# Layer 1's context values and keys, moved from the experts' stage to the first rows of block 2

## The chip, the cores and the metric

One core of one Trainium2 chip runs the whole program in one launch. The time is the device time in microseconds; a lower one is better. The engines are PE (TensorE, matmuls and transposes), ScalarE (ACT), VectorE (DVE), GpSimd (POOL), and SyncE (SP), which issues nearly all DMAs. Each engine works through its own instructions in a fixed order and waits on semaphores of the others.

## The reference

Two blocks of a network, one after the other, on 1024 latent rows and 256 context rows of width 1024, all in float32.

Block 1 mixes the latent rows (a Hyena filter and a gated linear recurrence, started from a context's states), adds the result, and then runs a mixture of experts over the latent rows:

```
aff = softmax(h @ router_w);  gates, idx = top_k(aff.T, 128)     # 16 experts, 128 rows each
y = (silu(xg @ w1) * (xg @ w3)) @ w2                             # w1, w3: 1024 x 2048, w2: 2048 x 1024
x = x + g2 * scatter_add(y * gates);  x = rmsnorm(x, final_g)
```

Block 2 has two layers. Each layer normalises the latent rows and a second context's 256 rows, projects them with `w_in` (1024 x 3072: Fourier and pool inputs, queries, keys, values, gate), lets the latent rows attend to the context's and the latent's keys and values, and adds the gated, projected result to the rows:

```
if update_ctx:  pc = hc @ w_in                        # layer 0
else:           pkv = hc @ w_in[:, K_OFF:G_OFF]       # layer 1: the context's keys and values alone
k_ctx = rms_norm(split_heads_qk(kc), qk_norm_g[1]);  v_ctx = split_heads_v(vc)
k_all = concat([k_ctx, k_lat]);  v_all = concat([v_ctx, v_lat])
```

Layer 1's context keys and values need the context rows after layer 0 and nothing of the latent rows. They are 256 x 512 each, in four heads of 128.

## The kernel before, in words

Matmuls of float32 precision are made of three: a matrix is split into a high half (`cp`, ScalarE) and a low half, the difference (`tt`, VectorE, or GpSimd where `eng` says so); `mm3` (lines 188 to 190) adds high x high, high x low and low x high in PSUM. A weight tile of 128 x 1024 is therefore loaded by SP (`wr`, `er`), copied by ScalarE (`wh`, `eh`) and subtracted by VectorE or GpSimd (`wl`, `el`) before PE can use it.

**The experts** (`moe`). For each of 16 experts `prep` gathers 128 rows by an indirect DMA of GpSimd, `up` makes a 128 x 512 block of both products from eight weight tiles each of `w1` and `w3` in four steps, `down` multiplies it by `w2`. Four such units an expert, 64 in all, read 768 weight tiles through `er` (10 buffers), `eh` and `el` (4 each). At an expert's end the two halves of `yo` are scaled on VectorE and added to `acc` in HBM by an indirect DMA of GpSimd (line 1265).

**The context beside them** (`ctx_rest`). `side_by_side` lays a second stream into the text of the experts: `ctx_rest` with a weight of 1/50 a step against 1/64 a step of the experts, so that its last step stands at some two fifths of them. It does layer 0's attention of the context, its output projection, which writes the new context rows to `xc` in HBM, and then the part that this document calls the tail: `ctx_hT(1)` loads `xc` (tile `cx`), normalises, transposes and scales it into `Tc`, high and low halves; `v_rows` makes the values of all heads from four weight tiles; `ctx_qk` makes the keys of a head from one weight tile each, normalises them and stores them. Its PSUM tiles are `cp` and `cm`, one bank each, its temporaries `cv` and `cu`, and its low halves are subtracted on GpSimd.

**Block 2's head.** `lat_pools` opens the weight and temporary tiles of the latent path (`wr` 2, `wh` 4, `wl` 4, `u2` 9) and PSUM (`pp` 3 banks, `pm` 1). `first_rows` then takes 256 rows at a time from `acc`: loads two tiles `r4`, squares them (ScalarE, into PSUM `fp`), scales them by `final_g` and stores them, normalises them again into `xn`, transposes them, and writes the halves to `T0`. `lat_path` follows: for layer 0 the values of the latent rows (`v_rows` with `rows_first`, four weight tiles held at once, two row tiles after two), then the queries and keys of each head, with the Fourier and pool work (`side_ct`) beside heads 1 and 2. Its `side_ct` tiles lie where those of `first_rows` were.

**Order.** The order of instructions on an engine isn't the program's. A scheduler goes through the program with a model of durations and puts on each engine's list the instruction that is ready first in the model, and among ready ones that which stands first in the program. Tiles of a pool that lies over a closed one's memory wait for the tiles that were there. The lists are fixed then; on the chip each engine keeps to its list.

Of the kernel before, what the change touches and what calls it, by code (L numbers as in the profile page):

```python
# [114 lines left out]
class Work:  # L115
# [1312 lines left out]
        self.dma(V, self.dvc[0, h])  # L1428
        return KA, lambda qb: (QA, QB), V, self.rqc[h]

    def ctx_qk(self, l, q, h, hT, w="w"):

        dst = self.dqc[h] if q == 0 else self.dkc[l, h]
        if q == 0:
            self.rqc.append(self.cst([128, 2, 2], name="rqc"))
        self.qk_rows(l, q, h, hT, 256, lambda t0, x: self.dma(dst, x), "cp", "cu", None, None if q else self.rqc[h],
                     w=w, eng=self.nc.gpsimd, pq="cm")

    def lat_operands(self, l, h):
        KA = [self.t("KA", [128, 1280], F32R) for _ in range(2)]  # L1440
# [362 lines left out]
    def ctx_rest(self):  # L1803

        dyc, dgc = self.dyc, self.dgc
        P_ = self.nc.gpsimd
        with ExitStack() as e:
            self.open(e, "right", cKA=4, cQA=6, cV=2, cE0=2, cE1=2, cth=2, cot=1)
            s0 = self.cst([128, 4, 2], name="s0")
            for h in range(4):  # L1810
                yield from self.attention(0, 256, 256, self.ctx_operands(h), dyc[4 + h], s0[:, h], "c")
        with ExitStack() as e:
            self.open(e, "right", cy=4)
            y = self.gated_y(0, 0, dyc, dgc, s0, "cp", "cy", "Tc", "cv")
            gb = self.t("cy")
            self.dma(gb, self.m2[0, 1, 2 * D:].partition_broadcast(128))
            xs = []
            for i in range(2):
                x = self.t("cy")
                self.dma(x, self.I["ctx_2"][0, i * 128:i * 128 + 128, :])  # L1820
                xs.append(x)
            yield
            for u in range(4):
                us = slice(u * 256, u * 256 + 256)
                wp = [self.wsplit(self.I["w_out_2"][0][q * 512:q * 512 + 512, us].rearrange("(k p) n -> p k n", p=128), (4, 256), "w", P_) for q in range(2)]
                for i in range(2):
                    is_ = slice(i * 128, i * 128 + 128)
                    ps = self.ps("cp", [128, 256])
                    for k in range(8):
                        wh, wl = wp[k // 4]  # L1830
                        self.mm3(ps, y[0][k // 4][:, k % 4, is_], y[1][k // 4][:, k % 4, is_], wh[:, k % 4], wl[:, k % 4], k == 0, k == 7)
                    t = self.t("cu", [128, 256])
                    self.tt(t, ps, gb[:, us], MUL)
                    self.tt(xs[i][:, us], xs[i][:, us], t, ADD, P_)
                    if u == 3:
                        self.dma(self.xc[i * 128:i * 128 + 128, :], xs[i])
                    yield
        with ExitStack() as e:
            self.open(e, "right", cx=2)
            hT = self.ctx_hT(1)  # L1840
            yield
        self.v_rows(1, 256, hT, self.dvc[1], "cp", "cv", "w", P_)
        yield
        for h in range(4):
            self.ctx_qk(1, 1, h, hT)
            yield

    def new_hT(self, tag):
        return [[self.t(tag, dt=F32R) for _ in range(8)] for _ in range(2)]
# [98 lines left out]
def side_by_side(*streams):  # L1948

    todo = [[-lead / total, total, list(gens)] for lead, total, gens in streams]  # L1950
    while todo:
        s = min(todo, key=lambda t: t[0])
        g, w = s[2][0]
        if next(g, todo) is todo:
            s[2].pop(0)
            if not s[2]:
                todo.remove(s)
        else:
            s[0] += w / s[1]


def run(K):
    fst = ExitStack()
    with ExitStack() as e1:
        K.open(e1, "left", ar=3, ah=4, al=4)
        K.open_ps(e1, "left", pp=3, mp=1)
        K.open(e1, "left", u2=4, T=16)
        K.open_ps(fst, "right", pf=4)
        K.open(fst, "right", f4=7, fb=5)
        with ExitStack() as e2:  # L1970
            K.open(e2, "right", cr=6, x=4, c=2, mr=4)
            K.start()
        K.open(fst, "right", y=3, t=4, H=2, hs=3, dc=2, ri=7, ra=2, mr=1)
        K.load_dft()
        K.mods_first()
        side_by_side((30, 450, [(K.filter_time(), 2.4), (K.filter_spectra(), 2.1), (K.hyena(), 5)]),
                   (0, 64, [(K.hy_proj(), 1), (K.hg_proj(), 1)]),
                   (0, 4, [(K.mods_layer(0, "mp", "u2", ("mr",), False), 1)]))
    fst.close()
    with ExitStack() as cx:  # L1980
        with ExitStack() as e1:
            K.open_ps(e1, "left", ph0=3, ph1=3)
            K.open(e1, "left", hmk=1, hS=2)
            for p in "01":
                K.open(e1, "left", **{"hi" + p: 6, "hw" + p: 5, "h2" + p: 3, "hm" + p: 4, "hT1" + p: 2, "hT2" + p: 4})
            K.ctx_state()
            for h in range(4):
                K.hgrn_head(h)
            K.open(cx, "right", wr=2, wh=2, wl=2, cu=6, cv=2, Tc=4, lg=2)
            K.pfx = "c"  # L1990
            with ExitStack() as e2:
                K.open_ps(e2, "right", cp=1, cm=1)
                K.open(e2, "right", mr=1)
                for _ in K.mods_tail("cm", "cv", ("wr", "wr", "mr"), False):
                    pass
                K.ctx_first()
                K.ctx_side()
                for _ in K.mods_layer(1, "cm", "cv", ("wr", "wr", "mr"), False):
                    pass
        K.open_ps(cx, "right", cp=1, cm=1)  # L2000
        K.pfx = "o"
        em = cx.enter_context(ExitStack())
        with ExitStack() as e0:
            K.open_ps(e0, "left", pp=3, pq=2, pi=1)
            with ExitStack() as e1:
                K.open(e1, "left", xm=3, rw=1, wo=16, m4=3, yt=6, u2=3)
                K.out_proj()
            K.open(em, "left", el=4, eh=4, er=10)
            with ExitStack() as e1:
                K.open(e1, "left", twr=2, twh=2, twl=2)  # L2010
                K.open(e1, "left", aff=1, tk=12, tp=2, af=4)
                K.topk()
                K.pfx = "c"
                K.ctx_heads("tw")
        with ExitStack() as e1:
            K.open_ps(e1, "left", et=1, ea=3, ey=2)
            K.open(e1, "right", g2b=1, xg=1, xf=1, xh=4, sa=4, hh=4, yo=2)
            side_by_side((0, 64, [(K.moe(), 1)]), (CL, CT, [(K.ctx_rest(), 1)]))
    K.pfx = ""
    with ExitStack() as e1, ExitStack() as e0, ExitStack() as ec:  # L2020
        K.open(e0, "right", T0=16)
        rope = K.lat_pools(ec)
        hT = K.first_rows()
        K.lat_path(hT, rope, ec, e0, e1)


class Kern:
# [9 lines left out]
    def start(self):  # L2037
        W = self.work
        W.pc, W.psm, W.pd, W.one = self.pc, self.psm, self.pd, self.one
        run(W)  # L2040
# [119 lines left out]
```

## Time and profile before

| | |
|---|---|
| time, median of 3 runs | 3869.8 us (3867.06 to 3873.09) |
| the profiled execution | 3865.27 us, span 3863.5 us |
| PE busy in the span | 3548.4 us (92%) |
| VectorE, ScalarE, GpSimd busy | 2722.9, 2224.8, 1125.8 us |
| HBM | 669.00 MB read, 107.05 MB written, 201 GB/s over the span |
| experts' weights asked for by SP | from 1183.7 to 2508.2 us |
| the tail's work on the rows `cx` and `Tc`, and its last store of keys | 1581.3 us to 1747.2 us |
| first and last matmul of layer 0's latent values | 2552.6 to 2613.7 us |

Times in rows are microseconds from the start of the span. `x` before a number counts instructions, unless it is the column of a matmul's shape. A matmul's duration in a row overlaps with the next one's; what a matmul costs PE is the distance from one start to the next. `<-` in brackets names what an engine waited for before an instruction, with the time it waited. PEld is PE's loading of weights, which overlaps with matmuls.

### The profile page before, as it was taken

The numbers are of one execution on the slowest core, as the hardware profiler recorded it, in microseconds if no ns is written. First come the engines' busy times: TensorE is split into PE (matmuls) and PEld (weight loads), VectorE is DVE, ScalarE is ACT, GpSimd is POOL, SyncE is SP. The second block draws the span as 40 slices with busy tenths as digits, with TensorE's granted clock in tenths as the row PEclk, the third lists the DMA queues.
The fourth block names the chain that finished last, engine by engine and source line by source line (L and its number), as shares of the span: only waits on it lengthen the run. The fifth ranks groups of instructions, "written<-read, shape, count | busy, mean of one in ns | idle before, by whom it ended". The sixth has DMA issues, their size and how long they took to land. (4 is left out here: it accounts for less than half of the span.)

```text
span 3863.5 us, 50949 instructions
## 1 busy us (share of the span) xinstructions
PE 3548.4 (92%) x17554; PEld 2851.0 (74%) x17554; DVE 2722.9 (70%) x4119; ACT 2224.8 (58%) x3595; POOL 1125.8 (29%) x702
## 2 busy tenths in 40 slices
PE   5998999968997899999999999979999899999989
PEld 2666878747866678787777777768778688877767
DVE  3588677787635888799888888856576744476762
ACT  4432322354434886777777777755576754456772
POOL 3355324364323213121112111001333610133361
PEclk8999999988997999999999999989999999999999
DMA  6765444363475799999999999952321143231133
GB/s 213 220 224 176 133 139 139 127 232 124 164 229 192 233 335 336 323 327 346 369 363 355 368 364 353 364 194 80 114 64 52 51 150 120 69 122 57 42 104 115
DMA packets 503020, 780.49 MB, mean 202 GB/s; under 512 B 35026, under 2 KB 238824, under 8 KB 502505
## 3 DMA queue, kind: packets, MB, share of 16 engines
q1 hardware_dynamic: 496136, 755.74, 57.3%
q0 software_dynamic: 5600, 20.43, 2.0%
q8 instruction: 138, 2.26, 0.2%
q10 hardware_dynamic: 1024, 1.06, 0.1%
q14 instruction: 122, 0.99, 0.1%
HBM read 669.00 MB, written 107.05 MB: 201 GB/s over the span
## 5 line engine op out<-in xcount | busy, mean ns | idle before, releaser
L171 DVE TENSOR_TENSOR el<-er,eh 128x1024 fp32r<-128x1024 f32 x763 | 950.6, 1294 | 112.5 <-ACT eh L168 109.4
L168 ACT ACTIVATE eh<-er 128x1024 fp32r<-128x1024 f32 x768 | 783.2, 1057 | 126.4 <-PE ea L190 92.7
L189 PE MATMUL ea<-el,xh 128*128 128x512 f32 x1024 | 415.8, 406 | 22.7 <-DVE el L171 20.2
L188 PE MATMUL ea<-eh,xh 128*128 128x512 f32 x1024 | 403.7, 397 | 1.9 <-ACT eh L168 1.9
L190 PE MATMUL ea<-eh,xh 128*128 128x512 f32 x1024 | 404.7, 395 | 0.0
L1488 DVE TENSOR_SCALAR_CACHE_REDUCE E<-s,rq 128x512 f32<-128x512 f32 (+1 forms) x384 | 237.3, 657 | 80.1 <-PE s L193 74.4
L1265 POOL DMA_INDIRECT acc<-yo,idx x16 | 71.1, 4444 | 733.8 <-DVE yo L180 726.7
L189 PEld LDWEIGHTS ea<-el,xh 128*128 128x128 f32 x1024 | 192.8, 188 | 91.3 <-DVE el L171 51.0
L165 ACT ACTIVATE E<-E,a 128x1280 f32<-128x1280 f32 x160 | 216.7, 1359 | 61.5 <-DVE a L1492 56.0
L193 PE MATMUL s<-KA,QA 128*128 128x512 f32 (+1 forms) x768 | 207.7, 394 | 32.2 <-DVE E L1488 31.1
L188 PEld LDWEIGHTS ea<-eh,xh 128*128 128x128 f32 x1024 | 192.9, 188 | 47.1 <-ACT eh L168 2.9
L190 PEld LDWEIGHTS ea<-eh,xh 128*128 128x128 f32 x1024 | 193.2, 189 | 37.6
L189 PE MATMUL ey<-el,hh 128*128 128x512 f32 x512 | 206.8, 404 | 6.4 <-DVE el L171 6.3
L188 PE MATMUL ey<-eh,hh 128*128 128x512 f32 x512 | 204.4, 405 | 7.4 <-ACT eh L168 7.3
L190 PE MATMUL ey<-eh,hh 128*128 128x512 f32 x512 | 203.6, 398 | 0.0
L171 POOL TENSOR_TENSOR wl<-wr,wh 128x1024 fp32r<-128x1024 f32 (+1 forms) x48 | 116.6, 2436 | 293.6 <-ACT wh L168 258.0
L168 ACT ACTIVATE u<-pp 32x512 f32<-32x512 f32 (+2 forms) x212 | 124.2, 586 | 112.1 <-PE pp L190 94.8
L193 PEld LDWEIGHTS s<-KA,QA 128*128 128x128 f32 x768 | 132.1, 199 | 74.6 <-DVE E L1488 55.0
L188 PE MATMUL pp<-T,ah 128*128 128x512 f32 x448 | 182.5, 407 | 2.0 <-ACT ah L168 2.0
L193 PE MATMUL po<-th,V 128*128 128x256 f32 x640 | 170.1, 391 | 13.7 <-ACT th L168 13.6
L190 PE MATMUL pp<-T,al 128*128 128x512 f32 x448 | 178.7, 399 | 0.0
L189 PE MATMUL pp<-T,ah 128*128 128x512 f32 x448 | 178.4, 398 | 0.0
(507 smaller groups left out, 8960.2 us busy)
## 6 DMA issues: line engine op xcount, KB each, us to landing
er<-in_exp_w_dram SPq DMA_DIRECT2D x768, 512.0 KB
wr<-in_w_in_dram SPq DMA_DIRECT2D x60, 512.0 KB
ar<-in_w_in_dram SPq DMA_DIRECT2D x64, 256.0 KB
mr<-in_w_mod_dram SPq DMA_DIRECT2D x30, 512.0 KB
wr<-in_ada_w_dram SPq DMA_DIRECT2D x24, 512.0 KB
wr<-in_w_out_dram SPq DMA_DIRECT2D x24, 512.0 KB
Hd<-hs SPq DMA_DIRECT2D x72, 128.0 KB
H<-Hd SPq DMA_DIRECT2D x36, 256.0 KB
```

The costliest lines, as they stand in the source:

```text
L165: return self.nc.scalar.activation(out, in_, func, **kw)
L168: return self.nc.scalar.activation(out, in_, AF.Copy)
L171: return (eng or self.nc.vector).tensor_tensor(out, a, b, op=op)
L188: mm(out, lh, rh, start=first, stop=False)
L189: mm(out, lh, rl, start=False, stop=False)
L190: mm(out, ll, rh, start=False, stop=last)
L193: self.nc.tensor.matmul(out, l, r, start=first, stop=last)
L1265: nc.gpsimd.indirect_dma_start(out=self.acc, out_offset=x[0], in_=yo, in_offset=None, compute_op=ADD)
L1488: nc.vector.tensor_scalar(E[:, k0:k1], o, r, None, op0=MUL, op1=ALU.min, accum_out=mx[:, m, j:j + 1] if nc_ > 1 else mc)
```

## The change

The tail leaves `ctx_rest`, which ends with the store of `xc`. It becomes a function of its own, `ctx_tail`, called behind `first_rows` and ahead of `lat_path` in the program. It uses the latent path's tiles (`pp`, `pm`, `u2`, `wr`, `wh`, `wl`) in place of the context's, with its low halves still on GpSimd. Two pools, `Tc` (4) and `cx` (2), 24 KB a partition, are opened below those of `first_rows` and closed behind the tail.

```diff
-    def ctx_qk(self, l, q, h, hT, w="w"):
+    def ctx_qk(self, l, q, h, hT, w="w", pt="cp", tmp="cu", pq="cm"):
...
-        self.qk_rows(l, q, h, hT, 256, lambda t0, x: self.dma(dst, x), "cp", "cu", None, None if q else self.rqc[h],
-                     w=w, eng=self.nc.gpsimd, pq="cm")
+        self.qk_rows(l, q, h, hT, 256, lambda t0, x: self.dma(dst, x), pt, tmp, None, None if q else self.rqc[h],
+                     w=w, eng=self.nc.gpsimd, pq=pq)
...
-        with ExitStack() as e:
-            self.open(e, "right", cx=2)
-            hT = self.ctx_hT(1)
-            yield
-        self.v_rows(1, 256, hT, self.dvc[1], "cp", "cv", "w", P_)
-        yield
+
+    def ctx_tail(self):
+
+        hT = self.load_h(self.xc, 256, self.A_2[1][:, 1], self.sh_2[1][:, 1], "Tc", "pp", "u2", "cx")
+        self.v_rows(1, 256, hT, self.dvc[1], "pp", "u2", "w", self.nc.gpsimd)
         for h in range(4):
-            self.ctx_qk(1, 1, h, hT)
-            yield
+            self.ctx_qk(1, 1, h, hT, "w", "pp", "u2", "pm")
...
         rope = K.lat_pools(ec)
-        hT = K.first_rows()
+        with ExitStack() as e2:
+            K.open(e2, "left", Tc=4, cx=2)
+            hT = K.first_rows()
+            K.ctx_tail()
         K.lat_path(hT, rope, ec, e0, e1)
```

## Rows read from the trace of the kernel before

**Rows 1.** Stretches: PE, PEld, DVE, ACT, POOL busy; clock, DMA share, GB/s.

```profile
1562.00:1750.00 188.00, 180.20 (x879) 147.87 (x878) 161.47 (x151) 144.32 (x190) 36.02 (x18) 0.97 0.94 320
1800.00:2500.00 700.00, 685.51 (x3010) 540.53 (x3009) 618.16 (x570) 530.24 (x614) 97.62 (x27) 1.00 1.02 361
```

**Rows 2.** The same stretches, PE's instructions on `ea` alone: busy, clock, DMA.

```profile
1562.00:1750.00 188.00, 107.68 (x415) 0.97 0.94 320
1800.00:2500.00 700.00, 454.82 (x1856) 1.00 1.02 361
```

**Rows 3.** The same for `ey`.

```profile
1562.00:1750.00 188.00, 53.92 (x192) 0.97 0.94 320
1800.00:2500.00 700.00, 232.47 (x926) 1.00 1.02 361
```

**Rows 4.** Waits, 1800 to 2500: who waited for whom, us, times, longest.

```profile
ACT eh L168 <- PE ea L190: 47.1, 89, 2.2
PEld ea L189 <- DVE el L171: 36.3, 59, 1.8
```

**Rows 5.** Groups by line and form, 1562 to 1750: count, busy us, mean ns.

```profile
L171 POOL TENSOR_TENSOR wl<-wr,wh 128x512 fp32r<-128x512 f32 x8 | 15.3, 1930 | 19.3 <-ACT wh L168 11.5 <-PE ey L190 7.7
L165 ACT ACT_TABLE_LOAD x8 | 10.3, 1283 | 0.1
...
L190 PE MATMUL cp<-Tc,wl 128*128 128x256 f32 x32 | 9.0, 281 | 0.0
...
L171 POOL TENSOR_TENSOR wl<-wr,wh 128x1024 fp32r<-128x1024 f32 x2 | 4.9, 2469 | 72.6 <-ACT wh L168 72.6
...
L196 PE MATMUL cp<-ident,cx 128*128 128x128 f32 x16 | 3.4, 294 | 0.2 <-ACT cu L165 0.2
...
L193 PE MATMUL cm<-cu,bd 128*128 128x256 f32 x8 | 2.4, 378 | 0.0
```

**Rows 6.** Timeline of PE: start, duration, what, idle time before it.

```profile
2549.04 3.92 PE L196 MATMUL fp<-ident,xn 128*128 128x128 f32 x16 [22.92 <-DVE xn L176]
...
2552.98 0.41 PE L189 MATMUL pp<-wl,T 128*128 128x256 f32 x1
2553.19 0.41 PE L188 MATMUL pp<-wh,T 128*128 128x256 f32 x1
...
2555.09 0.28 PE L189 MATMUL pp<-wl,T 128*128 128x256 f32 x1
2555.21 0.28 PE L190 MATMUL pp<-wh,T 128*128 128x256 f32 x1
...
2613.61 0.28 PE L189 MATMUL pp<-wl,T 128*128 128x256 f32 x1
```

**Rows 7.** Stretches at block 2's head, columns as in rows 1.

```profile
2526.00:2549.00 23.00, 0.12 (x1) 0.00 (x0) 9.55 (x13) 11.08 (x23) 1.55 (x1) 0.53 0.86 274
...
2550.00:2600.00 50.00, 45.47 (x349) 42.74 (x347) 31.27 (x65) 35.74 (x103) 0.35 (x2) 0.95 0.45 148
```

**Rows 8.** Timeline of ScalarE behind the last expert.

```profile
2526.33 1.06 ACT L168 ACTIVATE wh<-wr 128x1024 fp32r<-128x1024 f32 x1 [5.29 <-DMA wr<-in_w_in_dram]
...
2535.08 1.06 ACT L168 ACTIVATE wh<-wr 128x1024 fp32r<-128x1024 f32 x1 [4.56 <-DMA wr<-in_w_in_dram]
2537.41 0.60 ACT L165 ACTIVATE fp<-r 128x512 f32<-128x512 f32 x1 [1.28 <-DMA r<-acc]
```

**Rows 9.** Timeline of SP's DMA queue there.

```profile
2533.76 2.39 SPq L161 DMA_DIRECT2D r<-acc  x5
```

**Rows 10.** Timeline of GpSimd: two subtractions of the tail; the last scatter-add.

```profile
1673.43 4.50 POOL L171 TENSOR_TENSOR wl<-wr,wh 128x512 fp32r<-128x512 f32 x2
...
2527.19 1.55 POOL L1265 DMA_INDIRECT acc<-yo,idx  x1 [51.04 <-DVE yo L180]
```

**Rows 11.** Timeline of VectorE: three subtractions, beside the tail and alone.

```profile
1671.36 7.65 DVE L171 TENSOR_TENSOR el<-er,eh 128x1024 fp32r<-128x1024 f32 x3 [0.18 <-ACT eh L168]
...
2514.56 3.49 DVE L171 TENSOR_TENSOR el<-er,eh 128x1024 fp32r<-128x1024 f32 x3
```

## The prediction

> **What bounds the kernel now.** I read the busy time by stretches first, because the change takes work out of one stage and puts it into another, and the shares of the whole span say nothing about either. Two stretches of the experts' stage stand side by side [rows 1]: 1562 to 1750 us, in which the context tail (layer 1's context rows, values and keys) runs beside the experts, and 1800 to 2500 us, in which the experts run alone. In both PE is busy for about 96 to 98% and the DMA engines for 94 to 102%, so the reader cannot tell from busy shares what the tail costs. What tells it is progress: how many of the experts' matmuls PE got through. Alone the stage does 1856 up and 926 down matmuls in 700 us, 3.974 a us; with the tail beside it 415 and 192, 607 in 188 us, 3.229 a us [rows 2, 3]. At the rate of the stage alone 607 matmuls take 152.7 us. The tail therefore cost the experts 188 - 152.7 = 35.3 us.
>
> The waits of the stretch without the tail say which resource holds that rate [rows 4]. ScalarE waits for PE to give back a high half (47.1 us), PE's weight loads wait for VectorE's low half (36.3 us), and no engine is shown waiting for an expert weight to land. It is the hand-over round PE, at PE's pace, and not the DMA queue, although the queue looks full.
>
> The second stage is the beginning of block 2. The timeline of PE [rows 6] shows it standing still for 22.92 us between the last expert's matmul and the first transpose of block 2: last result, scatter-add [rows 10], reload of the rows [rows 9], two normalisations [rows 8]. After that PE is busy for 45.47 of 50 us [rows 7]: the matmuls of layer 0's latent values, which follow the rows as they come, fill it until 2613.5. So there are about 22.9 + 4.5 = 27.4 us of PE idle here, most of it in one piece.
>
> **The change, part by part.** *Out of the experts' stage.* Six groups of 32 matmuls with 256 columns, 0.118 us from start to start at the full clock (2555.09 to 2555.21) [rows 5, 6], are 192 x 0.118 = 22.7 us; 16 transposes 1.9 (an estimate: half of the 0.245 us each that 16 take at the half clock [rows 6]), the key norms' eight records 2.4: 27.0 us of PE. The rest of the 35.3 us is what it does to the hand-over: eight table loads of ScalarE, 10.3 us, because the tail's square roots alternate with the experts' Silu [rows 5], and a VectorE held up by GpSimd (below). Lower bound 27 us (PE time alone), upper 36 (the whole lost progress, plus two weight splits that lay ahead of 1562). I take **34 us**: the experts' own rate behind 1750 is seen in this trace and nothing else runs there, so I am near the measured loss.
>
> *Into the head of block 2.* Where can it start? Its PSUM tiles (`pp`, `pm`) and weight tiles come from the pools of the latent path, which lie over the experts' own, so it can't start before the experts give those back; its two row tiles lie beside them and can be loaded earlier. ScalarE does its last expert copy at about 2521 and is idle for 5.29 us [rows 8]. The granted clock in the idle stretch is 0.53 [rows 7], so PE starts there at the lower of its two levels, 1.2 of 2.4 GHz. From there: one normalisation, half of the 11.6 us that two took from 2537.41 [rows 8] to 2549.04 [rows 6], 5.8 us; then transposes at the slow clock, 16 in 3.92 us [rows 6]. PE starts the tail near 2528 and has all its rows near 2537.
>
> The weights are slower than the rows. All go through the two `wr` tiles: four tiles of values, four of keys, and only then the four for layer 0's latent values, which had the ring to themselves before. In the trace a wr tile's copy on ScalarE starts at 2526.33 and the third, which needs the first one's buffer back, at 2535.08, 8.75 us later [rows 8]: load, copy 1.06, subtraction 1.22 on VectorE. With the tail's subtraction on GpSimd (2.47 us for a value tile, 2 x 1.93 for a key tile [rows 5]) a buffer's round is about 10 to 11 us, and two buffers give a tile every 5.2 us. The first is usable at 2530 (2526.33 + 1.06 + 2.47), the second 3 us later, the third about 2538.5, the fourth waits on SP behind the five row loads of 2533.76 [rows 9] and comes near 2545. The 96 value matmuls then end near 2550: half of them at full clock 5.7 us, the others partly at the half clock, where the step is 0.21 us (2552.98 to 2553.19) [rows 6]. So the transposes and values lie inside the old 22.92 us of idle. The keys come at 2548, 2553, 2558 and 2564, and their 11.4 + 2.4 us of PE lie behind it. The latent values' weights follow; I put the first pair at 2571. In that time PE also does the first rows' transposes, as before.
>
> From there 384 latent value matmuls x 0.118 = 45.3 us, and about 4 us of transposes and gaps: they end near 2621, where they ended at 2613.6 before [rows 6]: 7 us. The path over the first rows gives a second end: their last part was ready near 2602 (2613.6 less 96 x 0.118), and may become up to 7 us later without being felt. I take **8 us**, one for small things. Bounds: 0 if all of the tail fits into the 27.4 us of idle, 27 if nothing of its PE time does.
>
> *GpSimd against VectorE.* In the tail of before, VectorE's three subtractions at 1671.36 took 7.65 us, while GpSimd ran its two at 1673.43; three alone took 3.49 [rows 10, 11]. So the tail's eight splits, 4 x 2.47 + 4 x 3.86 = 25 us of GpSimd, now meet the first rows' VectorE work. If each costs the first rows its whole length, they are 25 us late, 2613.6 + 25 is the end, and the cost is 25 in place of 8: that is a rival, below. But VectorE was busy for only 9.55 + 31.27 us of the 73 us in the two stretches of [rows 7]; it has the room, and 7 us of delay are free, so I add nothing. The Trainium skill (SBUF — State Buffer, "SBUF: two separate sides") has this as an exclusive lock on a port pair that VectorE and GpSimd share: whichever starts first holds it for its whole instruction. This trace agrees, with 7.65 against 3.49 us; by that rule in full the cost would be the 25 us of the rival.
>
> *Other moves.* The two row loads, the eight weight loads and eight stores stand in SP's queue among the latent path's; the five row loads of the first rows wait for the scatter-add, so what stands behind them there waits with them, and I have counted it for the fourth tile. The square roots now stand among other square roots: the table loads go. The side work's weight tiles, which lie over the tail's `Tc` tiles, are first loaded behind 2590, after the tail. Pushing the first rows' tiles up by 24 KB puts them over experts' tiles that end with the scatter-add for which they wait anyway. All that costs nothing; without this cover each would be one load's wait, 5 us.
>
> **The sum.** The profiled execution took 3865.3 us, span 3863.5. 3865.3 - 34 + 8 = 3839.3. The median of the runs is 3869.8, 4.5 us above that execution, so the median should come to **3844 us**.
>
> **Rivals.** *The DMA queue holds the experts' stage* (10%). For it: the DMA share of 1.02 [rows 1]. Against it: no wait on a landing [rows 4]. Then only bytes count: eight tiles of 128 x 1024 f32 (0.52 MB), two row tiles and eight small stores, 6.3 MB, at 361 GB/s 17 us. 3865.3 - 17 + 8 + 4.5 = 3861.
>
> *The weight ring* (14%): the two wr buffers turn more slowly than I have it, so that twelve tiles before the latent values make PE wait and nothing of the tail is hidden. For it: two buffers, and a round of 8.75 us that was already longer than its parts. Against it: two loads are always on the way. 34 gained, 27 lost: 3863.
>
> *Slower* (8%): in the queues' fixed order the tail stands ahead of the first rows' transposes, and the ring serves one tile at a time. One mechanism: PE can't pass a key matmul that waits for its weights, so block 2 begins when the twelfth tile has come. At 8.75 us a tile that is 12 x 8.75 = 105 us behind 2521, 2626, where the latent values began at 2553 before: 73 us late, of which 16 are won back, since from 2553 to 2613.6 they had 61 us for 45.3 us of matmuls. 3869.8 - 34 + 57 = 3893. It decides from a loss of 34 + 8 us, a tile every 7.5 us. Against it: PE ran transposes and value matmuls by turns as each got ready, so the order isn't the program's [rows 6, 7].
>
> *VectorE behind GpSimd* (6%): the first rows give up all 25 us of the tail's splits, worked out above: 3869.8 - 34 + 25 = 3861. That the change does nothing, the tail running beside the experts as before, is excluded: its PSUM isn't free until they end.
>
> **How the numbers follow.** The forecast has 62%; its own range is 3834 (36 gained, 0 lost) to 3855. A difference of 0.2%, 7.7 us, is about what a measurement of this kernel can tell from none. Faster by more than that is below 3862: all of the forecast, and some two thirds of the DMA, ring and GpSimd cases (30% together), rounded down: 0.8. Same: the other third of them, 0.12. Slower: the slow case, 0.08. The range is 3832 to 3864: it takes in the three nearer rivals and leaves out the slow one.
>
> **What would show it.** In the changed profile: no `Tc` work between 1562 and 1750, and the experts at about 3.97 matmuls a us there; the last expert matmul near 2492 instead of 2526; the eight table loads gone; the old 22.92 us of idle broken up by `pp` matmuls on `Tc`; the latent values ending some 94 us behind the start of the last scatter-add, where it was 86.4 (2527.19 to 2613.6). The prediction is wrong if the experts' last matmul moves by less than 25 us (step one), or if the latent values end more than 105 us behind the scatter-add (step two).

## The result, and the profile after

The changed kernel takes 3893.07 us (median of 4 runs, 3889.14 to 3899.96); the kernel before, run beside it, 3868.43. The ratio is 1.0073, 95% interval 1.0059 to 1.0087: 25 us slower by the medians, where 26 us faster were forecast. The profiled execution has a span of 3887.4 us, 23.9 more than before.

Two differences make these 23.9 us. The last scatter-add of the experts starts at 2485.53 us, where it was 2527.19 [rows 10]: 41.7 us earlier. The latent values of layer 0 end at 2636.3, where it was 2613.6 [rows 6]; that is 150.8 us behind the scatter-add instead of 86.4: 64.4 lost. What follows the latent values takes 1251.1 us instead of 1249.9. -41.7 + 64.4 + 1.2 = 23.9.

**The experts are free of the tail.** The stretches, columns as in [rows 1] (busy us with counts of PE, PEld, DVE, ACT, POOL; clock, DMA share, GB/s):

```profile
1562.00:1750.00 188.00, 184.63 (x813) 146.01 (x812) 166.04 (x152) 144.82 (x169) 24.03 (x8) 1.00 1.03 371
1800.00:2450.00 650.00, 636.90 (x2797) 502.63 (x2796) 575.07 (x530) 492.62 (x568) 87.53 (x24) 1.00 1.02 361
2484.00:2507.00 23.00, 0.46 (x2) 0.03 (x1) 5.46 (x8) 10.10 (x23) 8.13 (x4) 0.54 0.79 251
2507.00:2560.00 53.00, 16.76 (x71) 13.96 (x72) 36.54 (x74) 36.01 (x108) 3.52 (x4) 0.50 0.32 111
2560.00:2590.00 30.00, 29.11 (x226) 27.61 (x224) 11.54 (x22) 15.78 (x37) 10.31 (x9) 0.98 0.48 139
2590.00:2640.00 50.00, 48.70 (x390) 47.58 (x391) 13.70 (x17) 13.35 (x23) 0.00 (x0) 1.00 0.44 129
```

The first of these stretches again, with the instructions on `ea` and then on `ey` alone (PE first, then PEld, DVE, ACT), as [rows 2, 3]:

```profile
1562.00:1750.00 188.00, 123.40 (x505) 93.07 (x503) 7.53 (x11) 6.61 (x11) 1.00 1.03 371
```

```profile
1562.00:1750.00 188.00, 62.05 (x247) 45.72 (x247) 2.98 (x4) 1.00 1.03 371
```

505 + 247 = 752 matmuls in 188 us are 4.00 a us, the 3.97 of the stage alone and not the 3.23 of before. The DMA share is 1.03 at that rate, so that the queue doesn't hold the experts to the rate of before.

**Block 2's head is not.** PE's timeline answers to [rows 6]: start, duration, what, idle time before it.

```profile
2484.06 0.40 PE L190 MATMUL ey<-eh,hh 128*128 128x512 f32 x1
2508.12 1.09 PE L196 MATMUL fp<-ident,xn 128*128 128x128 f32 x4 [23.66 <-DVE xn L176]
2510.78 3.10 PE L196 MATMUL fp<-ident,xn 128*128 128x128 f32 x12 [1.57 <-DVE xn L176]
2524.07 3.93 PE L196 MATMUL fp<-ident,xn 128*128 128x128 f32 x16 [10.19 <-DVE xn L176]
2538.62 3.92 PE L196 MATMUL fp<-ident,xn 128*128 128x128 f32 x16 [10.62 <-DVE xn L176]
2555.24 1.94 PE L196 MATMUL fp<-ident,xn 128*128 128x128 f32 x8 [12.69 <-DVE xn L176]
2556.97 0.85 PE L196 MATMUL pp<-ident,cx 128*128 128x128 f32 x3
...
2562.98 0.39 PE L188 MATMUL pp<-wh,Tc 128*128 128x256 f32 x1
...
2587.47 0.28 PE L190 MATMUL pp<-Tc,wl 128*128 128x256 f32 x1
2587.59 0.28 PE L188 MATMUL pp<-wh,T 128*128 128x256 f32 x1
...
2636.26 0.28 PE L190 MATMUL pp<-wh,T 128*128 128x256 f32 x1
```

The reader is to see three things. The 22.92 us of idle ahead of the first transposes are still there, whole (23.66). Behind them the first rows come 14.5 to 16.6 us apart, about as before, but between their transposes PE now stands still for 10 to 13 us each time, where the latent values ran before: 16.76 us of work in 53, at a granted clock of 0.50, the lower level, where [rows 7] had 45.47 of 50 at 0.95. And the tail begins only with the last of the first rows, so that three pieces of work stand one behind the other: the first rows to 2560, the tail to 2587.5, the latent values to 2636.3.

ScalarE's timeline, as [rows 8], shows how the tail came there:

```profile
2495.66 0.60 ACT L165 ACTIVATE fp<-r 128x512 f32<-128x512 f32 x1 [6.71 <-DMA r<-acc]
...
2548.91 0.60 ACT L165 ACTIVATE fp<-r 128x512 f32<-128x512 f32 x1 [1.61 <-DVE r L180]
...
2549.54 0.58 ACT L165 ACTIVATE fp<-r 128x512 f32<-128x512 f32 x1
2550.06 0.19 ACT L165 ACTIVATION_READ_ACCUMULATOR fp<-r 128x1 f32 x1
2550.15 0.58 ACT L165 ACTIVATE pp<-cx 128x512 f32<-128x512 f32 x1
...
2551.99 0.58 ACT L165 ACTIVATE fp<-r 128x512 f32<-128x512 f32 x1
```

The first square of the tail's rows stands on ScalarE's list inside the eighth and last normalisation of the first rows, behind two of its four squares (2548.91 and 2549.54; the third comes at 2551.99), and waits there for nothing: `cx` had been loaded at 1566. Ahead of the first rows ScalarE was idle for 6.71 us; a tail's square didn't stand there.

SP's queue shows what the latent values waited for. These are its loads of `wr` tiles behind the scatter-add:

```profile
2494.33 0.98 SPq L161 DMA_DIRECT2D wr<-in_w_in_dram  x2
...
2508.47 0.38 SPq L161 DMA_DIRECT2D wr<-in_w_in_dram  x1
...
2511.18 0.38 SPq L161 DMA_DIRECT2D wr<-in_w_in_dram  x1
...
2574.07 0.55 SPq L161 DMA_DIRECT2D wr<-in_w_in_dram  x1
```

From 2511.18 to 2574.07 no `wr` tile was loaded. ScalarE's next copy of a weight tells why:

```profile
2570.73 1.15 ACT L168 ACTIVATE wh<-wr 128x512 fp32r<-128x512 f32 x2 [3.98 <-PE pp L190]
```

The tail's four value tiles were split by 2511 and held all four `wh` and `wl` until PE had used them; two key tiles filled both `wr`; the latent values' tiles stood behind those.

### The profile page after: what moved, and what is told of

Read it like the earlier page. It is cut to its first block, busy times and chain, and to the rows that moved or that the text cites. A ratio compares the mean times of both kernels' runs of the same rounds, so it can differ in the third digit from the quotient of the medians.

```text
span 3887.4 us, 50959 instructions
## 1 busy us (share of the span) xinstructions
PE 3544.4 (91%) x17554; PEld 2844.1 (73%) x17554; DVE 2715.0 (70%) x4119; ACT 2216.8 (57%) x3587; POOL 1128.1 (29%) x702
## 5 line engine op out<-in xcount | busy, mean ns | idle before, releaser
L171 DVE TENSOR_TENSOR el<-er,eh 128x1024 fp32r<-128x1024 f32 x763 | 936.8, 1280 | 108.2 <-ACT eh L168 104.5
```

Of the source, the lines that this page charges most:

```text
L171: return (eng or self.nc.vector).tensor_tensor(out, a, b, op=op)
```

## The experiments

My theory had two parts. **S:** a tail called behind the first rows is late because of small tiles. `row_rstd` takes `s2` and `ss`, four buffers each, and the first rows, ahead in the program, take eight `s2` before the tail takes one. **H:** once the tail is late, its value tiles hold the weight ring, and the latent values can't run beside the first rows. The rival **T:** the tail is late merely because it stands behind in the program.

What the traces showed, in us behind the start of the last scatter-add (which is at 2527.2, 2485.5, 2485.8, 2487.0, 2490.5, 2483.9, 2482.7 and 2491.5 in this order), with the medians and the ratio to the kernel before, run beside each (3868.43 us for the changed kernel, 3867.3 for e1 to e4, 3866.1 for e5 and e6):

| kernel | tail's first square | tail's last key matmul | last transpose of first rows | latent values end | median, us | ratio, 95% |
|---|---|---|---|---|---|---|
| before | in the experts | in the experts | 72 | 86 | see above | |
| after | +65 | 102 | 74 | 151 | 3893.07 | 1.0073 (1.0059 to 1.0087) |
| e1 own small tiles | -10 | 48 | 95 | 110 | 3850.92 | 0.9958 (0.9945 to 0.9972) |
| e2 no tail | | | 76 | 90 | 3832.28 | 0.9912 (0.9897 to 0.9927) |
| e3 tail first | -10 | 47 | 89 | 104 | 3842.94 | 0.9930 (0.9916 to 0.9943) |
| e4 latent values first | +74 | 117 | 73 | 86 | 3867.09 | 0.9994 (0.9984 to 1.0003) |
| e5 e3, VectorE splits | -10 | 40 | 91 | 106 | 3854.97 | 0.9972 (0.9960 to 0.9984) |
| e6 e4 with own small tiles | +74 | 117 | 74 | 86 | 3859.79 | 0.9983 (0.9974 to 0.9992) |

**e1, small tiles of the tail's own.** The tail stays where it is in the program; its small tiles get a name of their own, and so buffers of their own.

```diff
             hT = K.first_rows()
+            K.pfx = "c"
             K.ctx_tail()
+            K.pfx = ""
```

> The changed kernel, with other names for the tail's small tiles alone (sums of squares and roots: cs2 and css in place of s2 and ss, which the first rows use). Theory S: the four buffers of s2 and ss are given out in the program's order, and the tail's come behind the eight of the first rows, so its first square had to wait for their last one (2550 us). Then with own names the first square on cx runs within 10 us of the experts' last copy, at 2475 to 2490, the values' matmuls stand inside the idle time ahead of block 2's first transpose, and the time is 3868 - 42 + 8 to 20 = 3834 to 3846. Rival T: the tail is late because it stands behind the first rows in the program. Then nothing changes: first square near 2550, 3893 us.

Measured: 3850.92 us, 42 less than the changed kernel, by two lines that change no arithmetic and no order in the program. The tail's rows are squared 74 us sooner, ahead of the last scatter-add:

```profile
L165 ACT ACTIVATE pp<-cx x4: 577/582/603, 2475.8 to 2478.6; 128x512 f32<-128x512 f32 x4
```

```profile
L188 PE MATMUL pp<-wh,Tc x32: 278/283/583, 2490.2 to 2518.9; 128*128 128x256 f32 x32
```

The second row is the tail's values. They begin 4 us behind the scatter-add, in the idle time that the forecast gave them, but end 33 us behind it, where the forecast had 23 (2550). S holds and T falls: the place in the program is the same. The time is somewhat above the range expected.

The names themselves came with the change. Among the experts the tail's small tiles carried the prefix `c` too; the call behind `first_rows` stands where the prefix is empty, so that the tail took the first rows' `s2` and `ss` without a line that says so. The first of these rows is from the kernel before, the second from the changed one, where one of the nine is the tail's (the kernel before has eight):

```profile
1601.81 0.29 ACT L165 ACTIVATE css<-css,eps 128x2 f32<-128x2 f32 x1
```

```profile
L165 ACT ACTIVATE ss<-ss,eps x9: 278/295/296, 2499.6 to 2554.5; 128x2 f32<-128x2 f32 x9
```

What e1 doesn't tell is whether the number of buffers or the order in which one name is given out held the tail. By the number, four, the tail's `s2` needs only the fifth normalisation's to come back, and in the changed kernel VectorE read that one at 2532.30:

```profile
2532.30 0.16 DVE L171 TENSOR_TENSOR ss<-s 128x2 f32<-128x2 f32 x1 [0.18 <-ACT fp L165]
```

The tail's first square came 18 us later, right behind the eighth normalisation's first two. That fits the order better than the number; more buffers under one name weren't tried.

**e2, no tail at all.** Layer 1 reads the context's values and keys of layer 0; its own are not made.

```diff
-        self.dma(V[:, 0:2], self.dvc[l, h])
+        self.dma(V[:, 0:2], self.dvc[0, h])
...
-        self.dma(kc, self.dkc[l, h])
+        self.dma(kc, self.dkc[0, h])
...
-            K.open(e2, "left", Tc=4, cx=2)
+            pass
             hT = K.first_rows()
-            K.ctx_tail()
```

> The changed kernel without the tail: layer 1 reads layer 0's context values and keys in its place, and its two pools are not opened. What the experts' stage gives and what the rest of block 2's head takes without it. If all of the loss is the tail's and what it holds up: the experts end as in the changed kernel, the latent values end 86 us behind the last scatter-add as in the kernel before, and the time is 3868 - 42 = 3826 (3822 to 3831). If the head of block 2 became longer for another reason, it stays above 3840.

Measured: 3832.28 us. This is the floor, and it gives the tail's price in each place as a distance from it: 35 us among the experts (interval of the ratio, times 3867: 28 to 40), 61 in the changed kernel, 19 in e1.

**e3, the tail called first.**

```diff
+            K.ctx_tail()
             hT = K.first_rows()
-            K.ctx_tail()
```

> The changed kernel with the tail called ahead of the first rows, names as in it. Theory S: the tail's small tiles are then the first to be given out, so it starts behind the experts as in the run with own names, and the time is that run's within 8 us (3834 to 3854). Under rival T it starts there too, so this run does not tell S from T; it tells what it costs that the tail now goes ahead of the first rows wherever both are ready: over 8 us above the run with own names, if that matters.

Measured: 3842.94 us, the fastest of the kernels that do all the work, and 50 below the changed one. The price of the tail is 11 us. With the tail ahead in the program it takes its small tiles first, so no name is needed. The stretches from the scatter-add to the end of the latent values, columns as above:

```profile
2490.00:2513.00 23.00, 13.17 (x76) 11.75 (x76) 13.19 (x21) 14.41 (x35) 9.77 (x5) 0.78 0.84 263
2513.00:2536.00 23.00, 21.09 (x141) 19.28 (x140) 16.62 (x23) 18.18 (x48) 13.45 (x9) 0.87 0.74 241
2536.00:2594.00 58.00, 56.86 (x461) 55.55 (x461) 36.90 (x68) 36.07 (x92) 0.55 (x3) 0.99 0.53 165
```

PE is idle for 9.8 + 1.9 + 1.1 = 12.9 us here, where it was idle for 27.4 before [rows 6, 7]. The tail's 27 us of PE filled 14.5 us of idle; the other 12.5 are about the price measured, and about what the table shows (104 against 90 without a tail).

**e4, the latent values ahead of the tail.** They are called between the two, so that their weights come first in the ring.

```diff
-            self.dv = self.dram([4, 128, 8, 128], name="dv")
+            if l:
+                self.dv = self.dram([4, 128, 8, 128], name="dv")
...
-                    if h == l:
+                    if h == l and l:
...
             hT = K.first_rows()
+            K.dv = K.dram([4, 128, 8, 128], name="dv")
+            K.v_rows(0, 1024, hT, K.dv, "pp", "u2", rows_first=True)
             K.ctx_tail()
```

> The changed kernel with layer 0's latent values called between the first rows and the tail; small tiles still shared. Theory H, the second half of the loss: the tail is late, but what costs is that it holds the weight tiles wr, wh, wl, which the latent values behind it need, so PE stands still beside the first rows. Then with the values first they end 86 to 90 us behind the last scatter-add, as in the kernel before, the tail's 27 us of PE come behind them, and the time is 3868 - 42 + 27 = 3853 (3847 to 3860). If the late tail costs by itself and not by what it holds, the time stays near 3893.

Measured: 3867.09 us. The rows of the latent values and of the tail's keys:

```profile
L188 PE MATMUL pp<-wh,T x128: 274/281/562, 2512.1 to 2569.2; 128*128 128x256 f32 x128
```

```profile
L188 PE MATMUL pp<-Tc,wh x32: 280/283/283, 2588.6 to 2600.8; 128*128 128x256 f32 x32
```

H holds: with their weights ahead, the latent values run beside the first rows again and end 86 us behind the scatter-add, as they did before. The tail then stands alone, its last key matmul 31.6 us behind them; I had 27, its PE time, and missed the first of its weights, which come only when the latent values give the ring free. By the medians it costs 35 us, so that the experts' gain of 35 is paid back in full. Not all of that lies in the head: what follows the last key matmul takes 1260.9 us (span 3862.0 less 2601.1), where 1249.9 followed the latent values before. The cause of these 11 us stays open.

**e5, e3 with the low halves on VectorE.**

```diff
-        self.v_rows(1, 256, hT, self.dvc[1], "pp", "u2", "w", self.nc.gpsimd)
+        self.v_rows(1, 256, hT, self.dvc[1], "pp", "u2", "w")
...
-                     w=w, eng=self.nc.gpsimd, pq=pq)
+                     w=w, eng=None if pt == "pp" else self.nc.gpsimd, pq=pq)
```

> The tail called before the first rows, as in e3 (3842.94 us, 11 us over the kernel without a tail), and the low halves of its twelve weight pieces made by VectorE instead of GpSimd. Three theories of the 11 us that are left. G: GpSimd's slow pieces hold the weight ring (1.3 to 2.8 us each, where VectorE takes 0.7 to 1.2): the latent values' weights come some 6 to 10 us sooner, they end 94 to 98 us behind the last scatter-add's start instead of 103.5, and the time is 3833 to 3838 us. R: the ring's order and TensorE's own work set it, whoever makes the low halves: within 4 us of e3, 3839 to 3847. D: VectorE is what the first rows need, and twelve pieces of 0.7 to 1.2 us, about 10 us, make them later: 3848 to 3854.

Measured: 3854.97 us, 12 above e3. The tail's keys end 6 us sooner behind the scatter-add than in e3, but not the latent values (106 against 104), so G falls. The time is the one that D gave, to a us, but D's reason isn't in the trace: the first rows end only 1.4 us later behind the scatter-add. What the trace shows lies behind the head: from the end of the latent values (2588.3, in e3 2594.0) to the end of the span (3846.0, in e3 3844.9) it takes 1257.7 us, where e3 takes 1250.9. Why these 7 us are lost stays open. The two profiled executions themselves (3848.0 and 3846.6 us) hide them: e5's is the fastest of its six, with an early end of the experts, and e3's the slowest of its five.

**e6, e4 with the names of e1.**

```diff
             K.v_rows(0, 1024, hT, K.dv, "pp", "u2", rows_first=True)
+            K.pfx = "c"
             K.ctx_tail()
+            K.pfx = ""
```

> Both edits at once: layer 0's latent values ahead of the tail, as in e4 (3867.09 us), and the tail's small tiles under names of their own, as in e1 (3850.92). If the late small tiles and the held weight ring were two independent losses, their gains over the changed kernel add: 42 + 26 = 68 us, 3825 us. My theory says that they don't: behind the latent values the tail's own weights come last, whenever its rows are ready, so only its normalisations and transposes (about 10 us of e4's tail) can move into the head, and the values and keys stand behind 2569 us as in e4: 3856 to 3866 us, the latent values ending 86 to 95 us behind the scatter-add's start and the tail's keys 25 to 30 us behind them. Then what the names gave in e1 was worth it because the tail's weights were first in the ring.

Measured: 3859.79 us, in the range of my theory; the intervals of e4 and e6 overlap, and their traces agree to a us. The two repairs don't add. But I also missed: I had the tail's squares early, and they come 74 us behind the scatter-add, as without the names. Something else that is given out in the program's order holds them; the three banks of `pp`, into which they write and which the latent values take first, are the candidate. ScalarE's timeline fits it: the latent values fill eight such tiles, and the tail's first square comes 3.6 us behind the copy that empties the sixth, with the first rows' work between; in e4 it is the same 3.6 us.

```profile
2562.22 0.60 ACT L168 ACTIVATE u<-pp 128x512 f32<-128x512 f32 x1 [0.66 <-PE pp L190]
...
2565.78 0.59 ACT L165 ACTIVATE pp<-cx 128x512 f32<-128x512 f32 x1
```

A run that gives the tail banks of its own wasn't made.

## Why the prediction was wrong

**Step one, the experts (34 us gained): right.** The scatter-add is 41.7 us earlier in the profiled execution, and in the eight profiled executions it stands at 2527 once and at 2483 to 2492 seven times, so each carries some 4 us. By medians e2, which differs from before in the experts by the same, gains 35. The eight table loads are gone (ScalarE has 3587 instructions, eight fewer). The rival by which the DMA queue holds the experts, with 17 us gained, falls with the 4.00 matmuls a us and these 35.

**Step two, "Into the head of block 2", failed, at its first question: "Where can it start?"** The prediction went through PSUM, weight tiles and row tiles and answered "PE starts the tail near 2528 and has all its rows near 2537", in the old idle time. In this kernel that would be some 42 us earlier, near 2486 and 2495; the tail's first transpose came at 2556.97. It left out the smallest tiles: `s2` and `ss`, of which four of each now serve both pieces of work; the section on the change, which names the tiles that the tail takes over, leaves them out as well. e1 shows that these alone held the tail: 42 of the 61 us.

**The term that this broke** was +8 for the head; measured +64. The rest of its working (ring, keys, latent values near 2571) rested on the start. Given the early start, as in e1 and e3, the tail's price was 19 and 11 us, within the prediction's own bounds of 0 to 27. So the estimate was one of another kernel, in which the tail does stand first. That e3's 3843 us is the forecast's 3844 is luck in part. By its trace the latent values end 104 us behind the scatter-add, 17 more than before and not the 8 of the forecast (94): the tail's values end 30 us behind it instead of 23, and the first rows' last transpose comes 17 us later than before (89 against 72), where 7 were allowed for. Against that, e3's median lies 4 us under its profiled execution, where the forecast put 4.5 on top.

**The ring.** I had twelve tiles pass at a steady pace and saw the danger only in that pace. It was instead that a tile is given back when PE has used it: four value tiles split by 2511 and used at 2563 to 2575 stopped all loads of `wr` for 63 us, where before the latent values' first tiles were copied at once [rows 8]. The rival "weight ring" named the place, not this; the slower rival gave 3893, the number that came, by a mechanism that did not: PE was never held by a key matmul, and the tail stood behind the first rows, not ahead of them.

**GpSimd against VectorE: small, as forecast.** GpSimd's and VectorE's timelines at the same moment, and VectorE's same two operations later, alone, answer to [rows 10, 11]:

```profile
2485.53 1.54 POOL L1265 DMA_INDIRECT acc<-yo,idx  x1 [51.02 <-DVE yo L180]
2486.55 5.20 POOL L171 TENSOR_TENSOR wl<-wr,wh 128x1024 fp32r<-128x1024 f32 x2
2505.08 5.09 POOL L171 TENSOR_TENSOR wl<-wr,wh 128x1024 fp32r<-128x1024 f32 x2 [13.34 <-ACT wh L168]
...
2571.44 5.04 POOL L171 TENSOR_TENSOR wl<-wr,wh 128x512 fp32r<-128x512 f32 x4 [4.80 <-ACT wh L168]
```

```profile
2505.43 5.30 DVE L176 TENSOR_SCALAR xn<-r,ss 128x1024 f32<-128x1024 f32 x2
...
2523.18 1.42 DVE L176 TENSOR_SCALAR xn<-r,ss 128x1024 f32<-128x1024 f32 x2
```

Two scalings took 5.30 instead of 1.42 us: 3.9 us lost, once, on the way to the first transposes. The rival's 25 us needed every subtraction to meet such work; of the eight tiles only the two at 2505.08 did; the keys' splits stand behind the first rows. The trace agrees here too with the exclusive lock that the Trainium skill describes (SBUF — State Buffer, "SBUF: two separate sides"): VectorE's pair of 5.30 us lasts about as long as GpSimd's of 5.09.

**What stays open:** why e1 is 8 us behind e3 (the table puts 6 of them into the first rows, and the latent values follow); the 7 us that e5, and the 11 that e4, lose behind the head; and whether `pp` held the tail in e4 and e6.

## What to carry to other kernels

Where moved work can start is decided by everything that it takes from a shared pool, the two-column tiles of a norm as much as PSUM and weights; list every tag that it shares with the work ahead of it in the program, also those that it takes over by a prefix that is set elsewhere. Here two such tags were enough to put the moved piece behind that work, with its data loaded 984 us earlier. And a weight tile split early for a late user isn't progress: it holds the ring for all that come behind.

## What the runs showed of the hardware that was not expected

GpSimd's subtraction of a 128 x 512 half of a key tile took 1.29 us here (eight in the stretch behind 2484), and 1.93 beside the experts [rows 5]; the key tiles' splits were priced by the slower one. PE's granted clock stayed at 0.50 from 2507 to 2560, though PE transposed 16 tiles every 14.5 to 16.6 us; where 16 ran in one piece they took 3.92 or 3.93 us, as at the start of [rows 6].

```profile
L171 POOL TENSOR_TENSOR wl<-wr,wh 128x512 fp32r<-128x512 f32 x8 | 10.1, 1292 | 8.0 <-ACT wh L168 8.0
```
